# One plain gate chunk fewer in the first feed-forward of a hybrid encoder block, its transposed input prepared in three steps in place of four

## The chip, the cores and the metric

The kernel runs on one core of a Trainium2 chip. The metric is the time of one execution in microseconds (us); what is compared is the median of the timed runs. The engines are TensorE (PE, matrix products, with PEld its weight loads), VectorE (DVE), ScalarE (ACT), GpSimd (POOL) and SyncE (SP, which issues the loads and stores).

## The reference, cut to what matters

One encoder block on 512 tokens of width 1024: a feed-forward, a mixer, a second feed-forward, each with an RMS norm ahead of it and behind it. All is float32. The part at hand is the first line.

```
def swiglu(h, w_gu, w_down):
    gate, up = jnp.split(h @ w_gu, 2, axis=-1)
    return (jax.nn.silu(gate) * up) @ w_down

h = h + 0.5 * rms_norm(swiglu(rms_norm(h, ffn1_pre_g), ffn1_w_gu, ffn1_w_down), ffn1_post_g)
h = h + rms_norm(mixer(rms_norm(h, mix_pre_g)), mix_post_g)
h = h + 0.5 * rms_norm(swiglu(rms_norm(h, ffn2_pre_g), ffn2_w_gu, ffn2_w_down), ffn2_post_g)
```

`w_gu` is 1024 x 5632 (gate and up beside each other, 2816 each), `w_down` 2816 x 1024.

## The kernel before, in words

**Precision by parts.** A float32 operand is split into a high part (a copy in the fp32r type, made by ACT) and a low part (the source less the high part, made by DVE); `split` (line 333) issues both. A product is three matmuls, high x high, high x low and low x high (`mm3`).

**Gate stage.** The gate and up products of a feed-forward run in 22 chunks of 128 columns of gate and as many of up, c = 0 to 21, all 512 tokens at once. Two forms of chunk stand one behind the other:

- *Plain chunks* (`gate_up`, line 407), c below `direct`. `load_gu` brings two weight tiles of 128 x 1024 and splits them. For each of the two halves (gate, up), 8 slices of the width and 3 products, one matmul of 512 columns goes to one bank of PSUM: banks (4 + 2c) and (5 + 2c) modulo 8. In the first feed-forward the input's norm is not applied ahead of the products; the row factors `rs` multiply the result. So three DVE operations and a Silu on ACT follow: `sil = pb0 * rs`, Silu, `sil = sil * rs`, `g = pb1 * sil`. Chunks 0 and 1 run on the raw input's parts while `rs` is still being worked out.
- *Winograd chunks* (`operands`, line 436, and `winograd`, line 462), c from `direct` to 21. The product of a 2 x 2 block of weight tiles and a 2 x 2 block of input tiles is made with seven products in place of eight. The weights' side needs four sums (S1 to S4) of 512 columns and splits of 1024 (parts 0 and 1), 512 (part 2, then S1 and S4 as 5 and 6) and 1024 (S2 and S3, parts 3 and 4) columns. The sums are made by DVE in the first two Winograd chunks, c below direct + 2, and by POOL after these. The seven products are 12 matmuls of 256 columns each, in this order by part and input: 0 with 11, 3 with T2, 1 with 21, 4 with T3, 5 with T1, 2 with T4, 6 with 22. They fill four banks from (4c) modulo 8 on. Five DVE operations and three on ACT combine them behind it. `operands(c + 1)` is written in the code right after chunk c's products.

**The transposed input's parts.** The Winograd chunks read seven operands made of the input (`B1`: 11, 21, 22, T1, T2, T3, T4), each of 1024 columns. First the input is scaled in place by gain and row factor (`scale`, eight DVE operations), then the four sums T1 to T4 are made in place (`sums`, DVE, 1024 columns each), and each of the seven is split (`put`: a copy on ACT, a subtraction on DVE). In place means an order: 11 is put before sum T1 overwrites it, T1 before T3 before T2 before T4, 22 before T2, 21 before T4. `steps1` (line 861) lists which of these are issued in the code behind which plain chunk (`after`, line 501).

**Buffers around it.** The operands of the Winograd chunks lie in three areas, `sets`, taken by `(21 - c) % 3`, and area 0 for c equal to `direct`: area 0 is free early, area 1 holds the raw input's parts and area 2 the plain chunks' weights, so both are free only once the last plain chunk is through. Their sums lie in one of two buffers, `sums[order(c)]`: the first is used by the plain chunks' results, so the first Winograd chunks all take the second. Their raw weights go through a ring of four buffers, of which the second also holds the gain that `scale` reads.

**Who sets the order.** Nothing of this runs in code order as such. Every operation is recorded (`Plan.add`), with what it must wait for by its data and buffers. `Plan.issue` then lays out the whole program: it simulates it forward with a cost for each operation, then backward to get each operation's latest start, and takes these as priorities for the next forward run; the best of six rounds becomes each engine's order. Each engine then runs its list in that order, and waits by semaphores. All operations therefore carry one line in the profile, L238.

After the gate stage the gates lie in DRAM, and the down projection reads them back.

Of the kernel before, what the change touches and what calls it, by code (L numbers as in the profile page):

```python
# [246 lines left out]
def hybrid_block(ctx, tc, A, out):  # L247
# [57 lines left out]
    def reg(o, n):  # L305
        assert R0 + o + n <= NCOL - N32
        return mem[:, R0 + o : R0 + o + n]
# [392 lines left out]
    def wino_steps(x, B, like):  # L700


        at = {"11": (0, 0), "21": (1, 0), "22": (1, 1), "T1": (0, 0), "T2": (1, 1), "T3": (0, 1), "T4": (1, 0)}

        def put(name):
            return lambda: split(like(B[name][0]), like(B[name][1]), x(*at[name]))

        def less(eng, a, b, out):
            return lambda: eng.tensor_tensor(x(*out), x(*a), x(*b), ALU.subtract)

        sums = {
            "T1": less(DVE, (0, 1), (0, 0), (0, 0)), "T3": less(DVE, (1, 1), (0, 1), (0, 1)),
            "T2": less(DVE, (1, 1), (0, 0), (1, 1)), "T4": less(DVE, (1, 0), (1, 1), (1, 0)),
        }
        return put, sums
# [133 lines left out]
    def pairs(spots):  # L849

        return {k: (reg(a, 1024), reg(b, 1024)) for k, (a, b) in spots.items()}

    his_los = mem[:, :7168]
    B1 = pairs({k: (8192 + 2048 * i, 9216 + 2048 * i) for i, k in enumerate(("11", "21", "22", "T1", "T2", "T3", "T4"))})

    def scale(k):
        return lambda: DVE.scalar_tensor_tensor(xraw[k], xraw[k], gcol[:, k : k + 1], rs, ALU.mult, ALU.mult)

    put, sums = wino_steps(lambda i, j: xall[:, 4 * i : 4 * i + 4, 256 * j : 256 * j + 256], B1,
                           lambda v: v.rearrange("p (k t) -> p k t", k=4))  # L860
    steps1 = {
        2: [scale(k) for k in range(8)] + [put("11")],
        3: [sums["T1"], put("21"), put("22"), sums["T3"]],
        4: [sums["T2"], put("T1"), put("T3"), sums["T4"]], 5: [put("T2"), put("T4")],
    }
    L1 = {
        "tmp": Ring([h[0], h[1]]), "sums": (hall[:, :2048], hall[:, 2048:]),
        "sets": (reg(22528, 7168), reg(0, 7168), his_los), "B": B1, "steps": steps1, "direct": 6,
        "own": {4 + u: {"to": (reg(22528 + 2048 * u, 1024), reg(23552 + 2048 * u, 1024))} for u in range(2)},
        "order": lambda c: 1 if c < 8 else (c + 1) % 2,  # L870
        "pairs": (3, 8, 4), "w_at": (0, 8192, 15360, -8192), "g_at": [(22528 + 2048 * i, 23552 + 2048 * i) for i in range(4)],
        "slots": (7168, 14336, 26624, 27648), "w_last": 8192,
    }
# [424 lines left out]
    def after2(n, t):  # L1298
        for hf in range(2):
# [7 lines left out]
    put, sums = wino_steps(lambda i, j: h4[:, 2 * j : 2 * j + 2, 4 * i : 4 * i + 4, :], B2,  # L1307
                           lambda v: v.rearrange("p (k n t) -> p n k t", k=4, n=2))
# [80 lines left out]
```

## Time and profile before

| what | value |
| --- | --- |
| median of 3 timed runs | 927.07 us (926.96 to 927.24) |
| profiled execution, its time | 926.21 us |
| its span, first to last instruction | 924.06 us |
| mean granted PE clock | 0.998 |
| gate stage of the first feed-forward: first 512-column matmul, first 256-column, last 256-column | 5.5, 72.3, 233.6 us |

All profile lines come from one execution. The span and what lies around it (2.15 us) make its time. In the table of the page's engines the share is busy time over the span; matmuls are pipelined, and their ends are modelled. A row of the timeline stands for one or several instructions of one kind in a row on one engine: its start, its length, the operation, the tiles written and read (m and memr are SBUF, psum is PSUM, gd is DRAM), the shapes, the count, and in brackets the idle time ahead of it with what ended it. Means of single instructions contain the tail that overlaps the next instruction; the distance of starts is what each takes of its engine.

### The profile page before, as it was taken

To read this page: it belongs to the slowest core of one execution; us is meant where nothing else is said; L and a number is where in the kernel's file an instruction comes from. 1 tells how busy PE (TensorE), PEld (TensorE's weight loads), DVE (VectorE), ACT (ScalarE), POOL (GpSimd) and SP (SyncE) were. 2 spreads that over 40 slices of the span, in tenths; PEclk is the share of its full clock that TensorE was granted. 3 is DMA by queue.
4 is the path that set the end of the run, shared out by engine and by line. 5 is a ranking of instruction groups with operands and counts; after the bars stand their busy time and mean duration, and the time that the engine had idled before them with its cause. 6 is when DMAs were issued, how large, how long until landed. Compare 5 with 4: busy or idle time off the path is not lost. (4 is left out here: it accounts for less than half of the span.)

```text
span 924.1 us, 15672 instructions
## 1 busy us (share of the span) xinstructions
PE 914.2 (99%) x5822; PEld 826.6 (89%) x5822; DVE 813.0 (88%) x1205; ACT 544.1 (59%) x972; POOL 357.3 (39%) x300
## 2 busy tenths in 40 slices
PE   9999999999999999999999999999999999999996
PEld 7889999999887788888978888999999999988785
DVE  7999999899999896588796678999998989999986
ACT  7446544544675674588777867655544444458562
POOL 0005777860300313222552323238787665130040
PEclk9999999999999999999999999999999999999999
DMA  7535354446534496314290115244434445464324
GB/s 259 171 114 183 115 145 142 158 124 221 171 126 149 114 268 181 63 57 93 93 190 26 46 46 180 94 171 162 144 119 144 131 126 180 142 208 145 114 69 159
DMA packets 65932, 128.02 MB, mean 139 GB/s; under 512 B 22337, under 2 KB 32449, under 8 KB 65857
## 3 DMA queue, kind: packets, MB, share of 16 engines
q1 hardware_dynamic: 64704, 125.20, 43.5%
q0 software_dynamic: 1008, 1.84, 1.2%
q8 instruction: 45, 0.74, 0.3%
q14 instruction: 31, 0.25, 0.1%
q10 hardware_dynamic: 144, 0.00, 0.0%
HBM read 107.36 MB, written 17.83 MB: 135 GB/s over the span
## 5 line engine op out<-in xcount | busy, mean ns | idle before, releaser
L238 PE MATMUL psum<-memr 128*128 128x256 f32 (+3 forms) x5480 | 894.0, 323 | 0.7 <-ACT memr L238 0.2
L238 PEld LDWEIGHTS psum<-memr 128*128 128x128 f32 x5480 | 788.4, 190 | 79.9 <-DVE memr L238 3.8
L238 POOL TENSOR_TENSOR m<-m 128x512 f32<-128x512 f32 (+7 forms) x255 | 318.1, 1263 | 491.5 <-DVE m L238 201.8
L238 ACT CAST memr<-m 128x1024 fp32r<-128x1024 f32 (+3 forms) x388 | 304.5, 811 | 223.8 <-PE psum L238 91.4
L238 DVE TENSOR_TENSOR memr<-m,memr 128x1024 fp32r<-128x1024 f32 (+4 forms) x379 | 405.0, 1098 | 17.8 <-ACT memr L238 16.9
L238 DVE TENSOR_TENSOR m<-psum,m 128x512 f32<-128x512 f32 (+4 forms) x199 | 125.0, 632 | 32.9 <-ACT m L238 22.6
L238 DVE TENSOR_TENSOR m<-m 128x512 f32<-128x512 f32 (+3 forms) x179 | 101.2, 589 | 3.6 <-DMA m<-in_ffn_w_down 0.5
L238 ACT CAST memr<-psum 128x512 fp32r<-128x512 f32 (+2 forms) x124 | 63.6, 522 | 31.2 <-PE psum L238 22.5
L238 DVE TENSOR_TENSOR memr<-psum,memr 128x512 fp32r<-128x512 f32 (+3 forms) x116 | 67.9, 603 | 12.5 <-ACT memr L238 11.3
L238 ACT COPY m<-psum 128x512 f32<-128x512 f32 (+3 forms) x98 | 45.4, 474 | 37.0 <-PE psum L238 34.6
L238 PE MATMUL psum<-m 128*128 128x128 f32 (+1 forms) x342 | 54.6, 279 | 2.1 <-DVE m L238 2.0
L238 DVE TENSOR_TENSOR psum<-psum,m 128x256 f32<-128x256 f32 (+1 forms) x86 | 49.9, 585 | 4.7 <-PE psum L238 3.1
L238 PEld LDWEIGHTS psum<-m 128*128 128x128 f32 x342 | 43.6, 155 | 10.0 <-DVE m L238 2.2
L238 ACT ACTIVATE m<-m 128x256 f32<-128x256 f32 (+3 forms) x88 | 41.4, 475 | 11.7 <-DVE m L238 11.5
L238 ACT ACTIVATE m<-psum 128x256 f32<-128x256 f32 (+2 forms) x62 | 27.4, 443 | 27.2 <-DVE psum L238 15.0
L238 DVE SCALAR_TENSOR_TENSOR m<-m 128x512 f32<-128x512 f32 (+1 forms) x36 | 32.2, 934 | 3.7 <-POOL m L238 3.2
L238 ACT ACTIVATE m<-psum,m 128x512 f32<-128x512 f32 x40 | 26.9, 687 | 7.7 <-DVE m L238 5.8
L238 POOL TENSOR_TENSOR memr<-m,memr 128x512 fp32r<-128x512 f32 (+1 forms) x14 | 23.2, 1673 | 14.1 <-ACT memr L238 7.7
L238 ACT ACTIVATE memr<-m 128x512 fp32r<-128x512 f32 (+2 forms) x28 | 20.9, 757 | 13.1 <-DVE m L238 11.6
L238 DVE TENSOR_REDUCE m<-psum 128x1 f32<-128x512 f32 x32 | 21.2, 682 | 2.0 <-PE psum L238 1.9
L238 ACT COPY psum<-m 128x512 f32<-128x512 f32 x28 | 16.3, 589 | 10.3 <-DVE m L238 10.0
L238 POOL CAST memr<-memr 64x512 fp32r<-64x512 f32 x8 | 5.9, 739 | 35.6 <-DVE memr L238 34.2
(26 smaller groups left out, 99.1 us busy)
## 6 DMA issues: line engine op xcount, KB each, us to landing
m<-in_ffn_w_gu SPq DMA_DIRECT2D x86, 512.0 KB
m<-in_ffn_w_down SPq DMA_DIRECT2D x44, 512.0 KB
gd<-m SPq DMA_DIRECT2D x44, 256.0 KB
m<-gd SPq DMA_DIRECT2D x64, 128.0 KB
m<-in_w_qk SPq DMA_DIRECT2D x8, 512.0 KB
h<-m SPq DMA_DIRECT2D x8, 512.0 KB
m<-in_w_out SPq DMA_DIRECT2D x8, 512.0 KB
m<-h SPq DMA_DIRECT2D x8, 512.0 KB
```

What stands on the lines that cost most here:

```text
L238: r = getattr(self.engines[eng], op)(*a, **k)
```

## The change

`direct` of the first feed-forward goes from 6 to 5: chunk 5 becomes a Winograd chunk. The list of steps behind the plain chunks then has three entries (2, 3, 4) in place of four: sum T1 moves behind chunk 2, sum T2 and part T1 behind chunk 3, and the parts T2 and T4, which stood behind chunk 5, behind chunk 4. The choice of the sums' buffer moves by one chunk. What is computed is the same.

```
     steps1 = {
-        2: [scale(k) for k in range(8)] + [put("11")],
-        3: [sums["T1"], put("21"), put("22"), sums["T3"]],
-        4: [sums["T2"], put("T1"), put("T3"), sums["T4"]], 5: [put("T2"), put("T4")],
+        2: [scale(k) for k in range(8)] + [put("11"), sums["T1"]],
+        3: [put("21"), put("22"), sums["T3"], sums["T2"], put("T1")],
+        4: [put("T3"), sums["T4"], put("T2"), put("T4")],
     }
     L1 = {
         "tmp": Ring([h[0], h[1]]), "sums": (hall[:, :2048], hall[:, 2048:]),
-        "sets": (reg(22528, 7168), reg(0, 7168), his_los), "B": B1, "steps": steps1, "direct": 6,
+        "sets": (reg(22528, 7168), reg(0, 7168), his_los), "B": B1, "steps": steps1, "direct": 5,
...
-        "order": lambda c: 1 if c < 8 else (c + 1) % 2,
+        "order": lambda c: 1 if c < 7 else c % 2,
```

With `direct` at 5, chunks 5 and 6 both take operand area 0 (chunk 5 by the rule for the first, chunk 6 because (21 - 6) % 3 is 0); chunk 5 fills the banks from 4 on, chunk 6 those from 0 on. POOL makes the sums from chunk 7 on, where it did from chunk 8 on.

## The prediction

> **What bounds the kernel now.** I read the page first, then a table of windows cut at the chunk borders of the first feed-forward, then the matmuls by form, and last VectorE's timeline around the border that the change moves. The page: engine totals, then PE, DVE and POOL in 40 slices of 23.1 us.
>
> ```profile
> span 924.1 us, 15672 instructions
> PE 914.2 (99%) x5822; PEld 826.6 (89%) x5822; DVE 813.0 (88%) x1205; ACT 544.1 (59%) x972; POOL 357.3 (39%) x300
> PE   9999999999999999999999999999999999999996
> DVE  7999999899999896588796678999998989999986
> POOL 0005777860300313222552323238787665130040
> ```
>
> TensorE (PE) is busy for 99% of the span: time goes only where matmul work goes, or where PE is made to wait. VectorE (DVE) is nearly as full in slices 2 to 10, the gate stage of the first feed-forward, and that stage is the one that the change touches. The windows (us, then PE, PEld, DVE, ACT, POOL busy, clock, DMA share, GB/s): one plain chunk, the last plain chunk, then the first three Winograd chunks.
>
> ```profile
> 50.56:61.44 10.88, 10.88 (x50) 9.01 (x48) 10.79 (x12) 4.31 (x5) 0.00 (x0) 1.00 0.46 152
> 61.44:72.32 10.88, 10.88 (x50) 9.01 (x48) 10.72 (x15) 5.33 (x7) 0.00 (x0) 1.00 0.26 94
> 72.32:82.40 10.08, 10.08 (x86) 10.08 (x85) 10.04 (x12) 5.81 (x10) 4.98 (x3) 1.00 0.60 178
> 82.40:92.48 10.08, 10.08 (x87) 10.08 (x86) 9.43 (x12) 6.53 (x11) 8.34 (x6) 1.00 0.56 185
> 92.48:102.56 10.08, 10.08 (x87) 10.08 (x86) 9.93 (x11) 5.31 (x10) 7.50 (x5) 1.00 0.36 130
> ```
>
> PE has no idle time in any of them, at full clock, and DVE has almost none either (10.72 of 10.88, 10.04 of 10.08). So the change shortens PE's work at a place where DVE must deliver the same operands earlier. The sum is therefore PE's saving less whatever DVE is late.
>
> **PE's part.** The matmuls of the last four plain chunks, and of all sixteen Winograd chunks, by form:
>
> ```profile
> L238 PE MATMUL psum<-memr 128*128 128x512 f32 x193 | 43.9, 389 | 0.0
> L238 PE MATMUL psum<-memr 128*128 128x256 f32 x1344 | 161.4, 283 | 0.0
> ```
>
> The mean of one (389, 283) contains the drain, which overlaps the next one; the step from one to the next is busy time less one drain over the count: (43.9 - 0.16)/193 = 0.2266 us and (161.4 - 0.16)/1344 = 0.1200 us. A plain chunk has 2 halves x 8 slices x 3 products = 48 matmuls of 512 columns, 10.88 us; a Winograd chunk 7 products x 4 slices x 3 = 84 of 256 columns, 10.08 us. The change removes one of the first and adds one of the second: **-0.80 us**, and nothing else in PE's work changes. [...]
>
> **DVE's part.** Here is its timeline from the transposed input's first part to the end of the first Winograd chunk (start, us, operation, count).
>
> ```profile
> 43.73 1.21 DVE L238 TENSOR_TENSOR memr<-m,memr 128x1024 fp32r<-128x1024 f32 x1
> ...
> 56.76 2.35 DVE L238 TENSOR_TENSOR memr<-m,memr 128x1024 fp32r<-128x1024 f32 x2
> 59.03 0.68 DVE L238 TENSOR_TENSOR m<-psum,m 128x512 f32<-128x512 f32 x1
> 59.63 1.22 DVE L238 TENSOR_TENSOR memr<-m,memr 128x1024 fp32r<-128x1024 f32 x1
> 60.76 2.01 DVE L238 TENSOR_TENSOR m<-m 128x512 f32<-128x512 f32 x3
> 62.69 2.43 DVE L238 TENSOR_TENSOR memr<-m,memr 128x1024 fp32r<-128x1024 f32 x2
> 65.03 1.82 DVE L238 TENSOR_TENSOR m<-m 128x1024 f32<-128x1024 f32 x2
> 66.94 0.69 DVE L238 TENSOR_TENSOR m<-psum,m 128x512 f32<-128x512 f32 x1
> 67.55 1.21 DVE L238 TENSOR_TENSOR memr<-m,memr 128x1024 fp32r<-128x1024 f32 x1
> 68.68 0.68 DVE L238 TENSOR_TENSOR m<-m 128x512 f32<-128x512 f32 x1
> 69.28 1.89 DVE L238 TENSOR_TENSOR memr<-m,memr 128x512 fp32r<-128x512 f32 x3
> ...
> 73.02 1.22 DVE L238 TENSOR_TENSOR memr<-m,memr 128x1024 fp32r<-128x1024 f32 x1
> ...
> 78.80 3.48 DVE L238 TENSOR_TENSOR memr<-m,memr 128x512 fp32r<-128x512 f32 x2
> 82.21 1.47 DVE L238 TENSOR_TENSOR m<-psum,m 128x512 f32<-128x512 f32 x2
> ...
> 85.88 1.02 DVE L238 TENSOR_TENSOR psum<-psum,m 128x256 f32<-128x256 f32 x2
> ...
> 88.07 0.69 DVE L238 TENSOR_TENSOR m<-psum,m 128x512 f32<-128x512 f32 x1 [0.42 <-ACT m L238]
> ```
>
> The last three rows are the five steps behind a Winograd chunk's products, four of 0.60 and one of 0.34: 2.75 us. One copy to the high part, on ACT, and the load that waits for the scalings:
>
> ```profile
> 62.81 1.05 ACT L238 CAST memr<-m 128x1024 fp32r<-128x1024 f32 x1 [0.71 <-DVE m L238]
> 43.88 0.33 SPq L238 DMA_DIRECT2D m<-in_ffn_w_gu  x1
> ```
>
> Steps of DVE, start to start: 1024 columns (59.03 - 56.76)/2 = 1.135 us, 512 columns 0.60 us (three in 1.89 with one drain). Read against the code, 60.76 is three sums of chunk 6's operands, 62.69 its two wide low parts, 68.68 its last sum and 69.28 its three narrow low parts: chunk 6's operands are whole at 71.17, 1.15 us ahead of its first matmul at 72.32, and 9.8 us ahead of the last product that needs them (six products of 1.44 us later). Its first parts, from the pair at 62.69, are there by 65.1 or sooner, 8.4 us ahead. Chunk 7's follow from 73.02 to 82.28, 8 to 10 us ahead of each product. Throughout the first Winograd chunks DVE runs about 8 us ahead of PE and no more.
>
> What the change takes from DVE is one plain chunk: two low parts of 1024 (2.27 us) and three operations behind the product (1.81 us), 4.08 us. From the first Winograd chunk on, DVE's list is otherwise the same list, one chunk number lower. PE gets there 10.88 us sooner. So each lead shrinks by 10.88 - 4.08 = **6.8 us**, and for the very first Winograd chunk, behind which the removed chunk's three operations stand, by 10.88 - 2.27 = 8.6 us: 8.4 becomes about -0.2 if the order stays. It need not stay. The planner sorts by latest start, and a tally by due time closes. From 43.73 DVE must do, by the second product at 61.44 + 1.44 = 62.88: the part 11, sums T1 and T3, part 22, sum and part T2 (six of 1.135 = 6.8), chunk 5's wide first part (1.1), three sums (1.8), its wide second part (1.1), and the operations behind chunks 2 and 4 (3.6): 14.5 us, done at 58.2. By the last product at 70.1 all of the input's parts, chunk 5's operands and chunk 3's three operations are due: 24.4 us and about 0.7 of idle steps, done at 68.8. For chunk 6 (begins 71.52) another 6.5 us: 75.3, against its last product at 80.2, or 78.1 when chunk 5's own results (2.75) go first. It closes with 1.3 to 5 us to spare, where there were 8 to 10. The sums now made earlier in the list cost nothing themselves: the same four sums and seven parts, only the code order in which the planner first sees them. T3's and T1's parts, due at 65.8 and 67.2 in the new order and made at 57 to 59 here, are what can step aside.
>
> Other edges: chunk 6 now shares its operand area with chunk 5, but each part is freed by a product 4 or more products before its successor needs it (5.8 us for a copy of 1.05 and a low part of 1.2). SyncE's queue carries the same loads of 512 KB, the removed chunk's two being replaced by chunk 5's operands; the one at 43.88 waits, as now, for the last scaling (DVE's step before 43.73), over 10 us ahead of the time at which the tally puts chunk 5's sums. One more chunk's sums go to POOL, which has time (7.5 of 10).
>
> The banks are the wait that the change adds. Chunk 4's two results lie in banks 4 and 5, and the first Winograd chunk now begins in bank 4, not 0. Its second product waits until DVE has read bank 5, a chain whose last step ran at 66.94 here, since nothing needed it. At its earliest it begins when chunk 4's last matmul ends, 61.5, and lasts 0.69: 62.2, before 62.88, if DVE is not inside a step of 1.1 us then. Bounds: nothing, or 0.5 us. I take 0.2, and 0.1 for small misfits at chunk 6; the cover is the 1.44 us of the first product and that PE may take products into banks 6 and 7 first.
>
> Sum: -0.80 + 0.3 = **-0.5 us**. The profiled execution took 926.21 us (span 924.06 and 2.15 around it), so 925.7; the median of the three timed runs is 927.07, 0.86 above it, so **926.6**. Later stages: DVE is behind by up to 4 us on entering the POOL phase, and must get it back before the down projection.
>
> ```profile
> 110.00:120.00 10.00, 10.00 (x86) 10.00 (x85) 9.86 (x11) 5.35 (x10) 7.41 (x4) 1.00 0.50 136
> 160.00:170.00 10.00, 10.00 (x86) 10.00 (x85) 8.65 (x11) 5.04 (x9) 9.10 (x6) 1.00 0.43 133
> 170.00:180.00 10.00, 10.00 (x86) 10.00 (x85) 8.64 (x12) 4.83 (x8) 7.50 (x5) 1.00 0.38 132
> 242.14 1.23 DVE L238 TENSOR_TENSOR memr<-m,memr 128x1024 fp32r<-128x1024 f32 x1 [1.97 <-ACT memr L238]
> ```
>
> It does: 1.3 us of every 10 are free from 160 to 180, and 2 us at 240, where it waits for a load.
>
> **The rivals.** *The lead runs out.* Until about 130 us DVE has 0.14 us free in 10 and cannot catch up. The smallest leads stand there, in chunks 11 and 12:
>
> ```profile
> 117.04 3.42 DVE L238 TENSOR_TENSOR memr<-m,memr 128x1024 fp32r<-128x1024 f32 x2
> 125.70 4.61 DVE L238 TENSOR_TENSOR memr<-m,memr 128x512 fp32r<-128x512 f32 x4
> ```
>
> The first pair's first half is chunk 11's second wide low part, done at 118.75, due 122.71 + 1.44 = 124.15: a lead of 5.4, and chunk 12's is 5.1. Less 6.8, PE would wait 1.7 us; once, as the wait itself restores the lead. Result -0.8 + 1.7 = +0.9: 928.0. For it: the step of a narrow low part grows from 0.60 to 1.7 us (the pair at 78.80) while POOL makes sums, so DVE's rate is set by both. Against it: in both chunks a narrow part due 5.8 us later was made first, and can be swapped. [...]
>
> *The banks decide* (the slower side). If chunk 4's last operation keeps its place in DVE's order, it ends at 67.63 - 2.27 = 65.4, and the product into bank 5 waits 2.5 us past 62.88. It decides as soon as that wait exceeds the saving by 1.85 us; -0.8 + 2.5 = +1.7, with a second late part +2.5: 928.8 to 929.6. Against it: the planner knows the bank's due time.
>
> *It does not do what it says.* The planner lays out the whole program anew, so stages far away may change order too. PE's idle time is 924.1 - 914.2 = 9.9 us in all, start and end included; I allow 0.7 us either way.
>
> **How the numbers follow.** Forecast 0.57; the lead runs out 0.22; the banks 0.12; a shift elsewhere that outweighs the rest 0.09. A measurement of this kernel tells about 0.2%, 1.85 us, from no change: faster means below 925.2, which needs all of the saving and over 1 us from elsewhere, 0.03; slower means above 928.9, half of the banks' case and a part of the two others, 0.14; within, 0.83. The range reaches from no wait with a good shift (926.3 - 0.7 = 925.6) to the banks' first price, 929.0.
>
> **What would show it.** Right: 128x256 matmuls begin near 61.4 us, 1428 in place of 1344, the gate stage ends near 233.1 in place of 233.6, with no PE wait over 0.3 us near 61 to 73. DVE's low parts are 1 to 4 us ahead of their products. Wrong: a PE wait named after DVE at 62 to 66 (banks), at 71 to 120 (lead), or a span that moves while the gate stage doesn't.

## The result, and the profile after

The changed kernel takes **936.88 us** (median of 4 runs, 936.07 to 938.10) where the kernel before takes 927.02 (926.54 to 927.24): a ratio of 1.0110, 95% interval 1.0098 to 1.0122. It is 9.9 us slower, and 7.9 above the upper end of the forecast's range. Its profiled execution took 937.65 us, 0.8 above its median; that of before was 0.8 below its own. A comparison of the two profiles therefore shows 11.4 us, 1.6 more than the medians.

The page of the changed kernel, with the lines that stand for before in the prediction, and TensorE's granted clock in the same 40 slices (23.4 us each):

```profile
span 935.8 us, 15745 instructions
PE 920.5 (98%) x5858; PEld 829.9 (89%) x5858; DVE 824.6 (88%) x1210; ACT 546.9 (58%) x977; POOL 363.5 (39%) x304
PE   9999999999999999999999999999999999999996
DVE  7999999999899988488797778899989989999986
POOL 0008657671400301242372322326866765240040
PEclk9999999999989999999999999999999999999999
```

TensorE has 36 matmuls more and 6.3 us more busy time, so part of the loss sits inside its busy time. Slice 12 of the clock (from 257 us) is the only one below 9. Cut at the stage marks (start of the first matmul of the next form, start of the down projection, its last matmul, first 256-column matmul of the second feed-forward):

| stretch | before, us | after, us | difference |
| --- | --- | --- | --- |
| start to the first plain matmul | 5.52 | 5.06 | -0.46 |
| plain chunks | 66.80 | 55.94 | -10.86 |
| Winograd chunks | 161.27 | 172.27 | +11.00 |
| down projection of the first feed-forward | 106.56 | 114.27 | +7.71 |
| its end to the second feed-forward's gate stage | 253.41 | 257.88 | +4.47 |
| the rest | 330.50 | 330.38 | -0.12 |

The gate stage, where the change was made, ends 0.32 us *earlier* than before. That is its earlier start (0.46 us) and no shorter stage: the plain and the Winograd row together are 0.14 us longer. The loss lies behind it, in two places. A span that moves while the gate stage doesn't is one of the prediction's own signs of being wrong.

*The down projection.* TensorE's timeline around 257 us; the bracket is the idle time ahead of a row and what ended it:

```profile
254.83 2.20 PE L238 MATMUL psum<-memr 128*128 128x512 f32 x9
257.22 0.73 PE L238 MATMUL psum<-memr 128*128 128x512 f32 x2 [0.19 <-DVE memr L238]
258.42 0.98 PE L238 MATMUL psum<-memr 128*128 128x512 f32 x3 [0.47 <-DVE memr L238]
260.69 7.51 PE L238 MATMUL psum<-memr 128*128 128x512 f32 x18 [1.29 <-DVE memr L238]
```

Three waits for a VectorE tile; measured from start to start they lengthen the steps by 0.35, 0.64 and 1.48 us. Then 18 matmuls take 7.51 us, where 18 x 0.2266 = 4.1 are due. The windows of 260 to 264 and 264 to 268 say why (PE, PEld, DVE, ACT, POOL, granted clock, DMA share, GB/s):

```profile
260.00:264.00 4.00, 3.31 (x7) 2.29 (x8) 3.96 (x6) 0.88 (x2) 0.00 (x0) 0.53 0.81 265
264.00:268.00 4.00, 4.00 (x12) 3.10 (x12) 3.60 (x7) 2.89 (x5) 0.00 (x0) 0.61 0.48 159
```

These are averages. Windows cut more finely show the clock at 0.50 from 260.28 to 267.11 us, so from within the third wait on, and at 1.00 on either side. Most 512-column steps there take 0.427 us in place of 0.2266; as an estimate, half of the 6.4 us from 260.69 to 267.11, 3.2 us, is lost. Before has no wait here, and a clock of 1.00:

```profile
260.00:264.00 4.00, 4.00 (x20) 3.30 (x19) 3.86 (x12) 1.53 (x3) 0.00 (x0) 1.00 0.45 158
264.00:268.00 4.00, 4.00 (x19) 3.34 (x18) 3.93 (x10) 3.29 (x6) 0.00 (x0) 1.00 0.74 216
```

The late operands are the second and third pair of down-projection weights: their last low parts end at 257.17 and 260.64, against 250.58 and 256.52 in before (read off by their place in VectorE's list). The first pair is 6.4 us late too (240.10 against 233.73), yet nothing waited for that. Ahead of the second pair VectorE is idle for 2.12 us, up to 252.00, as it was for 1.97 up to 242.14 in before: the 2 us at 240 that the prediction counted on are still a wait for a copy that waits for a load, and they give nothing back.

*The border to the mixer.* ScalarE's copy of the last mixer weight, first in before, then in the changed kernel, and TensorE behind it in the changed kernel:

```profile
339.64 1.05 ACT L238 CAST memr<-m 128x1024 fp32r<-128x1024 f32 x1 [0.98 <-DMA m<-in_w_v]
```

```profile
349.71 1.05 ACT L238 CAST memr<-m 128x1024 fp32r<-128x1024 f32 x1 [3.65 <-DMA m<-in_w_v]
```

```profile
355.32 1.46 PE L238 MATMUL psum<-m 128*128 128x128 f32 x8 [1.92 <-ACT memr L238]
```

The copy waits 3.65 us for the load, not 0.98, and TensorE then waits for ScalarE. From start to start its step is 2.09 us longer there, and 0.52 us at 352.67 for VectorE. The windows 354 to 358 and 358 to 362 have clocks of 0.73 and 0.84 behind that: 0.50 from 355.85 to 359.27, half of which, 1.7 us, is taken as lost. Together that is 4.3 of the 4.47 us of this stretch.

**Why VectorE was late.** In the prediction VectorE loses 6.8 us of its lead and wins it back from 160 us on. The windows that carried this, in the changed kernel:

```profile
160.00:170.00 10.00, 10.00 (x85) 10.00 (x85) 9.86 (x11) 4.72 (x8) 7.12 (x5) 1.00 0.40 133
170.00:180.00 10.00, 10.00 (x86) 10.00 (x85) 9.86 (x10) 4.71 (x8) 8.62 (x6) 1.00 0.45 134
```

VectorE is busy for 9.86 of each 10 us, where it was 8.65 and 8.64. The free time isn't there any more, although its list is the same. The groups of VectorE by form from 142.6 to 203 us, before and then after (count, busy us, mean ns of one):

```profile
142.60:203.00 60.40, 60.40 (x506) 60.40 (x505) 54.48 (x61) 30.31 (x51) 48.01 (x27) 1.00 0.45 140
L238 DVE TENSOR_TENSOR memr<-m,memr 128x512 fp32r<-128x512 f32 x19 | 20.7, 1106 | 0.0
L238 DVE TENSOR_TENSOR memr<-m,memr 128x1024 fp32r<-128x1024 f32 x13 | 19.2, 1475 | 0.0
POOL m L238 <- DMA m<-in_ffn_w_gu: 1.9, 1, 1.9
```

```profile
142.60:203.00 60.40, 60.40 (x505) 60.40 (x505) 59.52 (x62) 29.19 (x49) 44.18 (x27) 1.00 0.42 130
L238 DVE TENSOR_TENSOR memr<-m,memr 128x512 fp32r<-128x512 f32 x19 | 22.0, 1192 | 0.0
L238 DVE TENSOR_TENSOR memr<-m,memr 128x1024 fp32r<-128x1024 f32 x12 | 21.8, 1814 | 0.0
POOL m L238 <- DMA m<-in_ffn_w_gu: 14.4, 4, 5.0
```

(The last line of each is from the waits: in total, times, longest.) As many instructions, but the low parts have grown: 12 x (1.814 - 1.475) + 19 x (1.192 - 1.106) = 5.7 us, about all of the free 5.9 (60.40 - 54.48). The low part reads two SBUF tiles. POOL's sums run beside it for the same share of its time in both kernels (0.86 and 0.85 for the wide form), so it isn't that more of them fall onto it. What differs is which of the two starts first. First before, a low part that starts ahead of the sum; then the changed kernel, where the sum is already running:

```profile
151.34 1.22 DVE L238 TENSOR_TENSOR memr<-m,memr 128x1024 fp32r<-128x1024 f32 x1
151.51 2.19 POOL L238 TENSOR_TENSOR m<-m 128x512 f32<-128x512 f32 x1
```

```profile
160.83 1.74 POOL L238 TENSOR_TENSOR m<-m 128x512 f32<-128x512 f32 x1
161.35 2.31 DVE L238 TENSOR_TENSOR memr<-m,memr 128x1024 fp32r<-128x1024 f32 x1
```

In the first the low part takes its usual time and the sum is the long one. In the second the low part ends 1.09 us after the sum's end (160.83 + 1.74 = 162.57, 161.35 + 2.31 = 163.66), about its own length: it waits for the sum. So it is wherever a low part starts behind a running sum in this stretch of both profiles (1.08 to 1.09 us after its end for the wide form, 0.54 to 0.56 for the narrow one; up to 1.20 and 0.61 where the sum had 0.1 us or less left). Counted so, the low parts wait 11.9 us for POOL's sums in this stretch in before and 17.4 in the changed kernel, 5.5 us more: the growth of 5.7, nearly.

Why the order turned is only read off the waits. POOL's own wait for raw weights went from 1.9 to 14.4 us, and SyncE's queue waited 55.8 us for VectorE's low parts where it was 37.9: VectorE, being late, gives the raw buffers back late, the next loads are late, and POOL's sums with them. That this is what puts a sum ahead of a low part is argued, not shown; no run changes the order of starts by itself. The lead of the first wide low part of a chunk over its product: before, about 8 us in chunks 6 to 12, then growing to 12.7 in chunk 17 and 15.3 in chunk 21; after, 1.4 in chunk 8, 3.5 in 10 to 14, 2.8 in 17, 6.2 in 21. The last low part of chunk 21 ends at 222.27 in place of 213.10, and all that VectorE does for the down projection stands behind it.

That was read off the two profiles. The theory to test (**theory 1**): VectorE enters the last chunks late, can't recover while its low parts wait for POOL's sums, and the down projection pays. Rivals: the new phase of the buffer rings; the three-step list; a plan laid out anew, whatever VectorE's load; and, for the border, the small loads beside the mixer weight.

### The profile page after: what moved, and what is told of

The parts are those of the page before. It is cut to its first block, busy times and chain, and to the rows that moved or that the text cites. A ratio compares the mean times of both kernels' runs of the same rounds, so it can differ in the third digit from the quotient of the medians.

```text
span 935.8 us, 15745 instructions
## 1 busy us (share of the span) xinstructions
PE 920.5 (98%) x5858; PEld 829.9 (89%) x5858; DVE 824.6 (88%) x1210; ACT 546.9 (58%) x977; POOL 363.5 (39%) x304
## 5 line engine op out<-in xcount | busy, mean ns | idle before, releaser
L238 PE MATMUL psum<-memr 128*128 128x256 f32 (+1 forms) x5516 | 900.4, 323 | 4.2 <-DVE memr L238 3.0
L238 POOL TENSOR_TENSOR m<-m 128x512 f32<-128x512 f32 (+5 forms) x259 | 324.1, 1268 | 495.8 <-DVE m L238 162.8
L238 ACT CAST memr<-m 128x512 fp32r<-128x512 f32 (+4 forms) x391 | 306.1, 810 | 229.4 <-PE psum L238 74.3
L238 DVE TENSOR_TENSOR memr<-m,memr 128x1024 fp32r<-128x1024 f32 (+4 forms) x382 | 412.0, 1110 | 19.3 <-ACT memr L238 18.4
L238 DVE TENSOR_TENSOR m<-m 128x512 f32<-128x512 f32 (+3 forms) x178 | 104.2, 607 | 2.7
```

Source lines behind the costliest of these rows:

```text
L238: r = getattr(self.engines[eng], op)(*a, **k)
```

## The experiments

The runs in one table: the end of chunk 21's last low part on VectorE, the length of the first down projection (both from the profiled execution), and the ratio to the kernel before run on the same chip (which took 926.54, 926.55 or 927.03 us there).

| run | last low part, us | down projection, us | median, us | ratio, interval |
| --- | --- | --- | --- | --- |
| kernel before | 213.10 | 106.56 | 927.02 | 1 |
| changed kernel | 222.27 | 114.27 | 936.88 | 1.0110, 1.0098 to 1.0122 |
| a1_rings | 223.09 | 114.98 | 938.15 | 1.0122, 1.0108 to 1.0136 |
| a2_less | 209.00 | 106.62 | 929.40 | 1.0027, 1.0016 to 1.0038 |
| a3_sums_dve | 218.32 | 109.06 | 930.39 | 1.0041, 1.0028 to 1.0053 |
| a4_dve_7_13 | 217.94 | 108.79 | 931.08 | 1.0050, 1.0038 to 1.0063 |
| a5_mix | 213.90 | 106.76 | 928.93 | 1.0031, 1.0022 to 1.0040 |
| a6_late | 221.91 | 112.33 | 934.08 | 1.0078, 1.0063 to 1.0093 |
| a7_less_late | 209.00 | 106.84 | 930.83 | 1.0044, 1.0029 to 1.0059 |
| a8_mix_late | 213.93 | 106.95 | 927.30 | 1.0008, 0.9998 to 1.0017 |
| b1_twice | 225.63 | 115.58 | 937.60 | 1.0119, 1.0105 to 1.0132 |
| b2_steps | 216.16 | 107.64 | 926.86 | 1.0007, 0.9997 to 1.0016 |
| b3_sums_dve | 210.29 | 106.66 | 926.37 | 0.9999, 0.9990 to 1.0008 |
| b4_twice_16_19 | 222.23 | 110.94 | 931.61 | 1.0052, 1.0037 to 1.0067 |

Read down the first two columns together: up to 213.9 us for the last low part the down projection takes 106.6 to 107.0 us, from 216 on it grows with the lateness, to 115.6 at 225.6. Only near 222 us do kernels with the same lateness differ, by up to 3.3 us.

**The ring phase.** One chunk fewer in plain form turns every ring of buffers by one chunk. Here they are turned back, in the changed kernel:

```
+                if rs is not None:
+                    raws.i += 2
+                    gates.get(), ups.get()
...
+                if rs is not None:
+                    raw4[0].i += 2
```

> The changed kernel with the three rings of buffers turned so that chunk 21 and the loads of the down projection use the same buffers as before the change (two raw buffers and one pair of result buffers further on). Theory 1 (VectorE comes about 9 us later to the down projection's operands, 222.8 in place of 213.0, because its lead never grows back): the loss stays, 934 to 940 us, PE waits again between 250 and 270 and at 350. Theory 2 (the rings' new phase makes the down projection's loads wait for chunk 21's buffers): the loss goes, 926 to 929 us, the first load of down weights is issued near 201 us as before.

Measured: 938.15 us, and waits of 0.85, 1.23 and 2.24 us at 256 to 259 us; the mean granted clock of its profiled execution is 0.992, where the changed kernel has 0.993 and before 0.998. The loss is all there, so the rival of the ring phase falls.

**Taking VectorE's lateness away.** In the changed kernel the wide low part of eight Winograd chunks, 12 to 19, is not made; the products read what an earlier chunk left there.

```
-            split(hi(0, 2), lo(0, 2), rg)
+            if rs is not None and 12 <= c < 20:
+                ACT.copy(r_(hi(0, 2)), rg)
+            else:
+                split(hi(0, 2), lo(0, 2), rg)
```

> The changed kernel without VectorE's low part of 1024 columns (parts 0 and 1) in chunks 12 to 19 of the first feed-forward; these products then read old low parts. It takes 8 steps of 1.13 us or, beside GpSimd, up to 2.3 us each, 9 to 18 us, from VectorE and nothing from PE. Theory 1: the loss goes, 926 to 928 us, VectorE starts on the down weights at 214 us or sooner. Theory 2: the loss stays, above 933 us.

Measured: 929.40 us. The last low part ends at 209.00, the down projection takes 106.62 us, as in before, with none of the waits at 256 to 259 and a mean granted clock of 0.997 (0.993 in the changed kernel). By the ratios this takes away 7.7 of the 10.2 us; the time is still 1.4 us above theory 1's range. What stays in its profile is 0.4 us up to the down projection's start, 1.4 in the mixer (a wait of 1.29 us at its border), 0.9 in the second feed-forward and 0.8 behind that.

**Adding the lateness alone.** The kernel before, six plain chunks and four steps as they are, with the same low part made a second time in the same chunks:

```
+            if rs is not None and 12 <= c < 20:
+                DVE.tensor_tensor(r_(lo(0, 2)), rg, hi(0, 2), ALU.subtract)
```

> The kernel before with VectorE's low part of 1024 columns made twice in chunks 12 to 19: 9 to 18 us more for VectorE, nothing for PE, rings and chunk forms untouched. Theory 1: PE stays whole through the gate stage and waits in the down projection, 933 to 940 us in all. Theory 2: 927 us, since no buffer has moved.

Measured: 937.60 us. The gate stage ends at 234.04, 0.45 us behind that of before, with one wait of 0.54 us in it; TensorE pays behind it, some 5 us ahead of the place in the changed kernel:

```profile
256.91 11.41 PE L238 MATMUL psum<-memr 128*128 128x512 f32 x39 [4.96 <-DVE memr L238]
```

```profile
256.00:260.00 4.00, 3.09 (x7) 2.51 (x8) 4.00 (x6) 0.13 (x2) 2.90 (x4) 0.50 0.59 158
```

One wait of 5 us, and a clock of 0.50 from 254.90 to 261.73: it fell 2.95 us into the wait. The mean of its wide low parts between 142.6 and 203 us is 1661 ns (1475 in before), and POOL waits 12.3 us for raw weights. So VectorE's lateness alone, with nothing of the change, makes a loss of the same size in the same stage, and longer low parts come with it. The border is another matter: the stretch behind the down projection is 1.0 us longer here, not 4.5.

**The list of steps alone.** The kernel before with the three-step list of the change, `direct` still at 6:

> The kernel before with the list of three steps alone: six plain chunks as before, only the code order in which the planner first sees the input's sums and parts is the changed one. Theory 1 (the lost lead of VectorE, which comes from the plain chunk taken out): no difference, 926 to 927.5 us. Rival: the new order of the sums and parts itself delays VectorE; then part of the 9.9 us shows here, above 929 us.

Measured: 926.86 us, ratio 1.0007 (0.9997 to 1.0016). By itself the list makes VectorE's last low part 3.1 us later (216.16) and the down projection 1.1 us longer, and the time stays within 0.2%; so the list alone doesn't make the loss, which comes with chunk 5's change of form.

**POOL's sums moved to VectorE.** First in the changed kernel, all chunks of the first feed-forward; then the same line in the kernel before.

```
-            eng = DVE if c < direct + 2 else POOL
+            eng = DVE if rs is not None or c < direct + 2 else POOL
```

> The changed kernel with all sums of the first feed-forward's Winograd chunks on VectorE, none on GpSimd. Alone, VectorE needs 4.08 + 2.41 + 2.75 = 9.24 us for a chunk of 10.08, where beside GpSimd it was busy for 9.86 in 10. Theory 1: the lead grows by some 0.8 us a chunk, the loss goes, 925.5 to 927 us. Theory 2: the loss stays, above 933 us. A third view, that VectorE simply has too much to do: 2.41 us a chunk more makes it worse than the change, above 938 us.

> The kernel before with all sums of the first feed-forward's Winograd chunks on VectorE. Theory 1: it had lead enough, so nothing on PE's path changes, 926 to 928 us; if the 3.8 us that the changed kernel still lost with its sums on VectorE come from VectorE's own load in the gate stage's first chunks, they don't show here; if they come from having no GpSimd help at the end of the gate stage, they show here too, near 930 us.

Measured: 930.39 us in the changed kernel, by the ratios 6.4 us less than the change alone; 926.37 in the kernel before, no difference. VectorE in the changed kernel so edited, from 142.6 to 203 us:

```profile
142.60:203.00 60.40, 60.40 (x505) 60.40 (x505) 59.94 (x90) 30.88 (x51) 0.00 (x0) 1.00 0.45 148
L238 DVE TENSOR_TENSOR m<-m 128x512 f32<-128x512 f32 x27 | 18.0, 681 | 0.0
L238 DVE TENSOR_TENSOR memr<-m,memr 128x1024 fp32r<-128x1024 f32 x13 | 15.8, 1216 | 0.0
L238 DVE TENSOR_TENSOR memr<-m,memr 128x512 fp32r<-128x512 f32 x20 | 13.5, 683 | 0.3
```

VectorE makes 27 sums more than before in this stretch, 16 us of work by its step of 0.60, and is still less late than in the changed kernel: a wide low part takes 1216 ns in place of 1814, a narrow one 683 in place of 1192. The lead grows by 0.9 us a chunk on average, from 3.0 us in chunk 11 to 12.0 in chunk 21. That is the recovery that the prediction counted on, and what had prevented it was POOL's sums. The time is no hit: 930.39 lies between theory 1's range (up to 927) and theory 2's (above 933), with the last low part still 5.2 us late. One wait of 1.38 us at 252, for ScalarE, is left in the down projection, and 1.43 at the border. In the kernel before, with its lead of 8 us, the same edit changes nothing: there the stretch is hidden.

**A part of the sums.** The changed kernel with VectorE's sums in chunks 7 to 13 alone:

```
-            eng = DVE if c < direct + 2 else POOL
+            eng = DVE if c < direct + 2 or rs is not None and 7 <= c < 14 else POOL
```

> The changed kernel with the sums of chunks 7 to 13 on VectorE and those of chunks 14 to 21 on GpSimd. Theory 1: the lead recovers in chunks 7 to 13 as with all sums on VectorE, and GpSimd then helps VectorE to the down projection's operands sooner (218.3 us for the last operand of chunk 21 with all sums on VectorE): 926.5 to 929.5 us. If GpSimd's sums cost VectorE their time in waiting wherever they stand: 930 us or more.

and with S1 and S4 of every chunk on VectorE, S2 and S3 on POOL:

```
-            eng.tensor_tensor(S1, a21, a22, ALU.add)
+            mixed = rs is not None and c >= direct + 2
+            (DVE if mixed else eng).tensor_tensor(S1, a21, a22, ALU.add)
...
-            eng.tensor_tensor(S4, a12, S2, ALU.subtract)
+            (DVE if mixed else eng).tensor_tensor(S4, a12, S2, ALU.subtract)
```

> The changed kernel with the sums S1 and S4 of chunks 7 to 21 on VectorE and S2 and S3 on GpSimd. Two sums each: VectorE alone needs 4.08 + 1.21 + 2.75 = 8.04 us a chunk, and half as many of its steps can be held up by GpSimd. Theory 1: the lead grows faster than with all sums on one engine, the loss goes, 926 to 929 us. If what costs is that the sums' chain passes between two engines: above 931 us.

Measured: 931.08 and 928.93 us. The first ends its last low part as late as the kernel with all sums on VectorE (217.94 against 218.32) and costs the same within the intervals; its time misses theory 1's range (to 929.5) and lies in the other view's, 930 us or more. The second is on time (213.90, down projection 106.76); at the other end TensorE waits 0.79 us at 66.03, for a bank of chunk 4. With the down projection back to within 0.2 us of before, 2.4 us are still missing, and 2.02 of them are in one wait at the border to the mixer. That made the border the next thing to test.

**The border.** The last in_w_v load takes 8.05 us in before from its issue to ScalarE's copy, and 10.69 in the changed kernel. In the changed kernel two loads of the relative position bias, of 32 KB each in packets of 128 bytes, are issued 0.4 us behind it (2.1 us in before). Here these are held back to a later part of the mixer, in three kernels: the changed one, the one without the low parts, the one with mixed sums.

```
+        if n == 2:
+            ACT.copy(tts[0][:, 0:1], h[1][:, 0:1])
```

(The copy writes into the buffer that the bias loads go to, so that they have to wait for it.)

> The changed kernel, in which the two loads of the relative position bias, issued 0.4 us behind the last load of in_w_v in the changed kernel, are held back until the mixer's first part is further on. At the border to the mixer ScalarE waited 3.65 us for that in_w_v load, and TensorE 2.09 us for ScalarE. Theory A, the bias loads share the DMA engines with the late load: ScalarE's wait falls to 2.0 us or less, TensorE's to below 1.3, and the time falls by 1 to 3 us, to 934 to 936. Theory B, the load is late because of what lies ahead of it: the wait stays between 3 and 4 us and the time at 936 to 938. Under both the waits of the down projection at 256 to 259 us stay, about 2.5 us together.

> The changed kernel without VectorE's wide low part in chunks 12 to 19 (their low parts are left stale), which ran at 929.4, and with the two loads of the relative position bias held back as in the run before. VectorE's lateness is gone from it, 1.3 us at the border to the mixer is left. Theory A, the bias loads make that wait: 928.0 to 928.6. Theory B: 929 to 930. If all that is lost is lateness and this border, A ends within 1.5 us of the kernel before.

> The changed kernel with two of the four sums of each Winograd chunk's operands on VectorE in place of GpSimd, which ran at 928.9 with a wait of 2.02 us at the border to the mixer, and with the two loads of the relative position bias held back. Theory A, the bias loads make that wait: 926.5 to 927.7, level with the kernel before. Theory B: 928.5 to 930.

Measured: 934.08, 930.83 and 927.30 us. ScalarE's waits at the border in the first, and in the last:

```profile
346.36 1.05 ACT L238 CAST memr<-m 128x1024 fp32r<-128x1024 f32 x1 [2.47 <-DMA m<-in_w_qk]
347.64 1.05 ACT L238 CAST memr<-m 128x1024 fp32r<-128x1024 f32 x1 [0.22 <-DMA m<-in_w_v]
```

```profile
341.69 1.05 ACT L238 CAST memr<-m 128x1024 fp32r<-128x1024 f32 x1 [1.97 <-DMA m<-in_w_v]
```

Theory A is right by its times in the first and the last, and its mechanism is seen in the last alone. With mixed sums the wait for in_w_v goes from 2.95 to 1.97, TensorE's wait of 2.02 us at the border is gone, and the ratio goes from 1.0031 to 1.0008, whose interval includes 1. In the changed kernel the wait for in_w_v goes from 3.65 to 0.22 us, and by the ratios 3 us are won (1.0110 to 1.0078). But ScalarE waits 2.47 us for an in_w_qk load in its place, 2.69 in all. Of the 3.7 us between the two profiles 1.9 are won in the down projection, ahead of these loads, where the waits come to 1.9 us (2.5 were to stay) and the clock of 0.50 lasts 3.4 us in place of 6.8 (0.57 on average from 260 to 264 us, 1.00 in the windows beside it); the other 1.9 are won behind it. The second is a miss for both theories: 930.83 where 928.0 to 930 was expected. Its plan puts an in_w_qk load ahead of the in_w_v one (as that of the first does), ScalarE waits 2.0 us for this, and TensorE has a new wait of 1.17 us for a POOL tile at 386.57 (0.60 at 390.41 in the first). So the held loads win something and cost something with each plan, and none of the three prices the small loads by themselves. In the 8 us around the in_w_v load the DMA engines are busy for a share of 1.00 in before (331 to 339 us) and 1.05 in the changed kernel:

```profile
339.00:347.00 8.00, 8.00 (x37) 6.63 (x36) 7.65 (x12) 3.79 (x10) 1.62 (x3) 1.00 1.05 254
```

Over the runs that load took 8.05 to 9.43 us with the bias loads 2.1 us behind it, 8.73 to 10.69 with them 0.4 to 0.6 us behind, and 8.57 to 8.76 with them held back. The ranges overlap, so the distance alone doesn't decide it. What else does stays open.

**Half the dose.** The kernel before with the low part made twice in chunks 16 to 19 alone (`16 <= c < 20` in the edit above):

> The kernel before, with the wide low part made a second time in chunks 16 to 19 only, half the dose of the run that made it so in chunks 12 to 19 and took 937.6. Theory 1, VectorE's lateness at the end of the gate stage is what costs, beyond what the start of the down projection can take: the last part of chunk 21 ends 4.5 to 7 us later than in the kernel before (213.1), at 217.5 to 220, the wait of TensorE near 252 is 0 to 2.5 us in place of 5.13, and the time is 927 to 932. A rival, that any addition to VectorE's list costs its own length wherever it stands: half of the 11.1 us lost with the full dose, 932 to 933. A second rival, that the plan moved and not the lateness: no relation to the dose, 935 to 938.

Measured: 931.61 us, inside theory 1's range. The lateness was mis-sized: 222.23 in place of 217.5 to 220, that is 9.1 us later than before with half the instructions, against 12.5 with all. By its time alone the rival "half of 11.1" isn't excluded either (4.6 us, 3.4 to 6.2 by the interval). But the run gives a better comparison than was planned: its last low part ends at 222.23, in the changed kernel at 222.27, and yet its down projection is 3.3 us shorter. Its TensorE around 260 us:

```profile
259.55 0.73 PE L238 MATMUL psum<-memr 128*128 128x512 f32 x2 [0.95 <-DVE memr L238]
260.68 7.50 PE L238 MATMUL psum<-memr 128*128 128x512 f32 x31 [0.40 <-DVE memr L238]
```

From the same instant, 31 matmuls run in 7.50 us, where the changed kernel had 18: 13 x 0.2266 = 2.9 us. The waits here come to 1.7 us in place of 2.5, and the granted clock stays at 1.00. Of the 7.7 us that the changed kernel loses in this stage, 2.5 are waits for VectorE there and 3.2 the half clock behind them; the rest is three waits of 0.3 to 0.9 us from 298 to 316 and steps a little longer.

## Why the prediction was wrong, step by step

- *PE's saving, -0.80.* Right: the plain chunks lose 10.86 us, the Winograd chunks gain 11.00, of which 0.9 is the wait below, so 10.1 is the new chunk. The 256-column matmuls begin at 61.0 (61.4 forecast), there are 1428, and the stage ends at 233.3 (233.1). This last hit is in part luck: the first matmul came 0.46 us earlier, and from there the stage is 0.14 us longer, not 0.5 shorter.
- *DVE's lead shrinks by 6.8.* Right: 8 to 1.4 us in chunk 8.
- *The tally by due time closes; banks 0.2, misfits 0.1.* Nearly. No wait at banks 4 and 5: TensorE runs unbroken from 59.64 to 74.1. There is one wait ahead of Winograd chunk 6's parts, 0.58 us, and 0.9 with the slower steps around it, where 0.3 was said to be the most; by its place it falls under the prediction's sign for the lead (71 to 120 us):

```profile
74.51 5.65 PE L238 MATMUL psum<-memr 128*128 128x256 f32 x45 [0.42 <-DVE memr L238]
```

- *"It does: 1.3 us of every 10 are free from 160 to 180, and 2 us at 240."* This is the step that failed. The free time was read from a VectorE that ran 8 us and more ahead, and was taken as a constant of its list. It came with that lead: once VectorE is late, its wide low parts take 1814 ns in place of 1475, as they start behind POOL's sums and wait for them (17.4 us in place of 11.9), and of the 5.9 us of slack in 60 only 0.9 are left. a3_sums_dve and a5_mix show that it recovers when POOL's sums are taken out or halved, b1_twice that a late VectorE costs the same without the change, a2_less that without the lateness the down projection is whole.
- *The place of the loss.* The prediction looked for the bill in the gate stage, and there it would have been 1.7 us. The bill came 24 us behind the end of this stage, where VectorE's list is full again (weights of the down projection, then the gates) and TensorE had no lead to live on.
- *The rival "lead runs out".* It had the right engine and the right reason: DVE's rate set by both. Its place, chunks 11 and 12, and its price were wrong, and "once, as the wait itself restores the lead" too: there was no wait in these chunks, so nothing restored it. The runs agree with that reason: 1216 ns for the wide low part and 683 for the narrow one without POOL's sums (a3_sums_dve), 1814 and 1192 beside them (the changed kernel). What the rival didn't foresee is that the price depends on which of the two starts first: a wide low part took 1.21 to 1.23 us where no sum was running at its start, and up to 2.32 us behind a running one.
- *The banks.* Not in the changed kernel: no wait at 62 to 66. But the wait is real: in a5_mix and a8_mix_late TensorE waits 0.79 and 0.78 us at 66 for chunk 4's last operation (66.22 to 66.91, it reads bank 5), a third of the 2.5 of that rival.
- *A shift elsewhere, 0.7 us either way.* Too small: the stretch from the down projection's end to the second feed-forward is 4.5 us longer. With the change but without the lateness (a2_less) it is 1.4 us longer, with the lateness but without the change (b1_twice) 1.0. Some 2 of the 4.5 us are in neither; what makes them isn't shown. a6_late, which holds two small loads back, wins 1.9 us in this stretch without showing that these loads were the cause.
- *The price of a wait.* It was counted at its own length. By the estimates above, the half clock behind it (0.50 for 6.83 and 3.42 us) added 3.2 us in the down projection and 1.7 at the border.

No version was faster than the kernel before. The best with five plain chunks, a8_mix_late, is level with it (1.0008, 0.9998 to 1.0017): PE's saving of 0.8 us is spent on the wait of 0.78 us for bank 5.

## What to carry to other kernels

Slack that a trace shows on an engine belongs to the state it was taken in: before spending it, look whether the instructions' means depend on a neighbour engine (two forms of one instruction, 0.60 and 1.7 us) and on how far ahead the engine runs: here the same low parts took 1475 ns on average with a lead of 8 us and more, and 1814 ns with one of about 3 (142.6 to 203 us of both profiles). When an edit takes lead from an engine, follow the lead to the next stage in which that engine's list is full, and not only to the end of the edited one. And price a wait of TensorE with what may follow it, not at its length alone: here a clock of 0.50 for 6.83 and 3.42 us followed some of the waits, and none followed others (b4_twice_16_19, a3_sums_dve).

## What the runs showed of the hardware

- **The clock after short waits.** In the changed kernel, waits that lengthen the steps by 0.35, 0.64 and 1.48 us within 4 us were followed by a clock of 0.50 for 6.83 us; in b1_twice it was 0.50 from 254.90 to 261.73 us, from within a wait of 5 us on. Behind the wait of 1.92 us at 353 to 355 us in the changed kernel it was 0.50 for 3.42 us. Waits of 1.16 and 0.56 us in b4_twice_16_19 and one of 1.38 us in a3_sums_dve left it at 1.00. What decides whether the clock falls isn't shown.
- **Who waits, a low part or a sum.** VectorE's step for 1024 columns was 1.135 us alone (two from 56.76 to 59.03 us in before). In the gate stage of before and of the changed kernel a wide low part with no sum of POOL running at its start took 1.21 to 1.23 us, and a sum that started inside it up to 2.21 us, where a sum beside no low part took 1.29 to 1.30. A wide low part that started while a sum was running ended 1.08 to 1.09 us after it (up to 1.20 where the sum had 0.1 us or less left) and took up to 2.32 us (the rows at 151 and 161 us above).
- **A full set of DMA engines.** With the 16 DMA engines busy for a share of 1.00 and 1.05, the last in_w_v load of 512 KB took 8.05 us in before and 10.69 in the changed kernel from issue to use.
